# Softmax of head pairs 0 to 6 divided behind the mixing, and the first output weights split by ScalarE and VectorE

## The chip, the cores and the metric

One core of a Trainium2 chip runs the whole program. The metric is the device time of one execution in microseconds, the median over repeated runs. The core has five engines, each with an in-order queue of its own: TensorE (PE; its weight loads are listed as PEld), VectorE (DVE), ScalarE (ACT), GpSimd (POOL) and SyncE (SP), which issues most of the DMAs.

## What is computed

Two layers on x of 512 frames by 1024 channels, in fp32: a causal pooling mixer with a gated MLP, then chunked attention with a gated MLP. The change lies in the attention (16 heads of 64 channels; with 512 frames and chunks of 64 a frame sees its own chunk and all before it):

```python
def chunk_attention(h, w_qkv, q_norm, k_norm, rel_table, w_o):
    q, k, v = jnp.split(h @ w_qkv, 3, axis=-1)
    q = head_rmsnorm(q, q_norm)
    k = head_rmsnorm(k, k_norm)
    ...
    s = jnp.einsum('bqhd,bkhd->bhqk', qc, kb) * scale + bias
    s = jnp.where(valid, s, -1e30)
    p = jax.nn.softmax(s, axis=-1)
    o = jnp.einsum('bhqk,bkhd->bqhd', p, vb)
    ...
    return o @ w_o

x = x + chunk_attention(rmsnorm(x, g), ...)
```

Softmax divides each row of exp(s - max) by its sum. The division may stand ahead of the product with v, where it acts on 512 x 512 numbers of a head, or behind it, where it acts on 512 x 64.

## The kernel before

Nearly every fp32 operand of a matmul is split into a high and a low part (`split`, lines 96 to 103: the high part is a rounded copy, by default by ACT, line 102, the low part is the difference, by default by DVE, line 103). With `eng_hi` and `eng` another engine does them (line 100 for the high part). A product is then three matmuls (`mm3`, lines 123 to 125: high by high, high by low, low by high). `load_split` (lines 111 to 119) loads a 128 x 1024 block of weights by SP's queue (line 117) and splits it; raw blocks have three buffers, high and low parts two each.

The attention works on pairs of heads, `p` 0 to 7, since two heads of 64 channels fill 128 partitions. One loop of 68 steps runs over the 64 tiles (head, 128 queries): in step i come the scores of tile i (`scores`), the transposition of tile i - 2 (`turn`), and every fourth step the mixing of a whole head whose last tile is i - 4 (`mix`). Two steps in eight also turn q and k of the next pair (`channel_major`). Between them PE is given "fillers": the projection of the next q and k (up to step 35.5), and from there the first six pairs' part of the output product (`outputs`, 144 matmuls), spread evenly over the steps.

For one tile the chain is: PE's `sc` (lines 1394 and 1395); DVE adds the bias and takes the extreme into `mx` (line 1398); ACT makes Exp into `sb` and its row sum (line 1400); DVE makes 1/sum (line 1401); ACT multiplies `sb` by it (line 1402); PE turns `sb` with `ident` into `tp` (line 1410); ACT and DVE split `tp` into `pt0h`, `pt0l` (even heads) or `pt1h`, `pt1l` (odd heads; lines 102 and 103); PE mixes into `oo` (line 1422); ACT copies half of it as `ob` (line 1427) and DVE adds it into `O2[p]`, named `o` in the trace (line 1428). `O2[p]` is split into `XS[p]`, named `two` in the trace, and multiplies the output weights `wo_h`, `wo_l`.

The order of PE alone is written by hand in this loop. On the other engines, SP's queue too, a scheduler lays the instructions out from the same program. `sc`, `zt`, `tp`, `oo` take the four buffers of the S bank of PSUM in rotation. The output weights of the first six pairs come in six blocks of 128 x 1024; POOL makes their high and low parts (`load` in `output`).

Of the kernel before, what the change touches and what calls it, by code (L numbers as in the profile page):

```python
# [17 lines left out]
F32 = mybir.dt.float32  # L18
F32R = mybir.dt.float32r
AF = mybir.ActivationFunctionType  # L20
# [3 lines left out]
P = 128  # L24
S = 512
# [5 lines left out]
HD = 64  # L31
NPAIR = H // 2
TT = S // P
# [39 lines left out]
def trunk(ctx: ExitStack, tc: tile.TileContext, xt, xT, cols, band, edge, poolw, gv, wout, wqk, wv, wo, rel, out):  # L73
    nc = tc.nc
# [3 lines left out]
    tmp = ctx.enter_context(tc.tile_pool(name="tmp", bufs=1))  # L78
    dram = ctx.enter_context(tc.tile_pool(name="dram", bufs=1, space=bass.MemoryType.DRAM))
# [9 lines left out]
    def psum(tag, name, bufs=2):  # L89
        return ps.tile([P, S], F32, name=name, tag=tag, bufs=bufs)  # L90
# [30 lines left out]
    def mm3(o, sh, sl, mh, ml, first, last, **how):  # L121

        yield nc.tensor.matmul(o, sh, mh, start=first, stop=False, **how)  # L123
        yield nc.tensor.matmul(o, sh, ml, start=False, stop=False, **how)  # L124
        yield nc.tensor.matmul(o, sl, mh, start=False, stop=last, **how)  # L125
# [15 lines left out]
    def small(name, n, tag="nw"):  # L141
        return tmp.tile([P, n], F32, name=name, tag=f"{tag}{n}", bufs=4)
# [211 lines left out]
    ident = consts.tile([P, P], F32, name="ident")  # L354
    col = consts.tile([P, NCOL], F32, name="col")
    ones = consts.tile([P, 1], F32, name="ones")
    gq = consts.tile([P, 2], F32, name="gq")
    rdram = dram.tile([H, RLEN], F32, name="rdram")
    ET = mybir.EngineType
    with tc.tile_pool(name="start", bufs=1) as sp, tc.manual_schedule(engines={ET.PE, ET.DVE, ET.Activation, ET.Pool, ET.SP}):  # L360
        first, second, acc0 = mixer(sp)

    def ffn(l, first, pool, acc, summed=None, upool=None, hook=None):
# [56 lines left out]
        def early():  # L420
# [6 lines left out]
            for at, (f, k, i) in enumerate(units):  # L427
# [13 lines left out]
                if at == (19, 14)[l]:  # L441

                    order = tc.manual_schedule(engines={ET.DVE, ET.Activation}) if l == 0 else nullcontext()
                    order.__enter__()
# [388 lines left out]
        def tour():  # L833
# [8 lines left out]
            def place(f, k):  # L842

                for word in PLACES[k].split():
                    x, name = word.split(".")
                    step = steps_of(f + "qofn".index(x) - 2).get(name)
                    if step:
                        step()

            for f in range(KIND.index("s"), NF + 2):  # L850
# [10 lines left out]
                for k in range(7):  # L861
                    if (f, k) == (ORDERED, 0):
                        order.enter_context(tc.manual_schedule(engines={ET.DVE, ET.Activation, ET.SP}))
                    place(f, k)
# [50 lines left out]
    def attention(rest, hook, hidden_slots):  # L915
        XS = set2
        O2, V, Z, QK, SM = {}, {}, {}, {}, {}
# [407 lines left out]
        def output(ps_, after=None):  # L1325

            p0, p1 = ps_[0], ps_[-1] + 1
            n = (p1 - p0) * P
            nd = D // n
            w = {}  # L1330

            def load(d):
                eng = nc.gpsimd if p0 < 6 else None
                w[d] = load_split(wo[d:d + nd, :, p0 * P:p1 * P].rearrange("d p m -> p d m"), D, f"wo{d}_{p0}", eng=eng, eng_hi=eng)

            o, early = {}, 2 if p1 - p0 == 4 else 0
            order = [(d, p) for d in range(early) for p in ps_[:-1]] + [(d, p1 - 1) for d in range(early)]
            for d, p in order + [(d, p) for d in range(early, KD) for p in ps_]:
                if d - d % nd not in w:
                    load(d)  # L1340
                hi, lo = w[d - d % nd]
                if d not in o:
                    o[d] = psum("PQ"[d % 2], f"wo{d}_{p0}")
                s = slice(d % nd * n + (p - p0) * P, d % nd * n + (p - p0 + 1) * P)
                yield from mm3(o[d], hi[:, s], lo[:, s], XS[p], XS[KD + p], p == p0, p == p1 - 1)
                if p < p1 - 1:
                    continue
                nc.vector.tensor_add(X[d], o[d], X[d])
                if after:
                    after(d)  # L1350
                    if d == 1:
                        load(nd)
# [28 lines left out]
        def scores(h, t):  # L1381

            p, e = divmod(h, 2)
            q, k, kl = QK[p, 0][e], QK[p, 1][e], KL[p % 2][e]
            if t == 0:

                base = rdram[h, :]
                for r, n in ((0, S - HD), (HD, S)):
                    nc.sync.dma_start(BT[h % 2][r:r + HD, S - n:], bass.AP(tensor=base.tensor, offset=base.offset + HD, ap=[[1, HD], [1, n]]))
            n = (t + 1) * P  # L1390
            nw = max(n, 256)

            sc = psum("S", f"sc{h}_{t}", 4)
            nc.tensor.matmul(sc[:, :nw], q[:, t * P:n], k[:, :nw], start=True, stop=False)
            nc.tensor.matmul(sc[:, :nw], q[:, t * P:n], kl[:, :nw], start=False, stop=True)  # L1395
            SM[h, t] = s_ = heads.tile([P, n], F32, name=f"sb{h}_{t}", tag=f"sb{t}")
            mx = tmp.tile([P, 3], F32, name=f"mx{h}_{t}", tag="mx", bufs=4)
            nc.vector.tensor_tensor_reduce(out=s_[:, :n], in0=sc[:, :n], in1=BT[h % 2][:, :n][:, ::-1], scale=1.0,  # L1398
                                           scalar=3e38, op0=OP.add, op1=OP.min, accum_out=mx[:, 0:1])
            nc.scalar.activation(s_[:, :n], s_[:, :n], AF.Exp, scale=-1.0, bias=mx[:, 0:1], accum_out=mx[:, 1:2])  # L1400
            nc.vector.reciprocal(mx[:, 2:3], mx[:, 1:2])
            nc.scalar.activation(s_[:, :n], s_[:, :n], AF.Copy, scale=mx[:, 2:3])

        def turn(h, t):

# [7 lines left out]
        def mix(h):  # L1413

            p, e = divmod(h, 2)
            hs = slice(e * HD, (e + 1) * HD)
            oo = psum("S", f"oo{h}", 4)
            if p not in O2:
                O2[p] = heads.tile([P, S], F32, name=f"o2_{p}", tag="o2", bufs=4)
            for c in range(2):  # L1420
                for j in range(TT):
                    nc.tensor.matmul(oo[:, j * P:], V[j, h // 4][:, h % 4].rearrange("p a d -> p (a d)"),
                                     PT[e][c][:, 4 * j:3 * j + TT].rearrange("p t q -> p (t q)"),
                                     start=j == 0 and c == 0, stop=j == TT - 1 and c == 1)
            ob = g_tile(f"ob{h}")
            other = slice(HD - e * HD, 2 * HD - e * HD)
            nc.scalar.activation(ob[hs], oo[other], AF.Copy)
            nc.vector.tensor_add(O2[p][hs], oo[hs], ob[hs])

        r2, late = small("r2", TT), []  # L1430
        closing = ExitStack()
        with tc.tile_pool(name="pre", bufs=1, reuse_waits="tile") as pre:
            with tc.manual_schedule(engines={ET.PE, ET.DVE, ET.Activation, ET.SP}):
                rcol, second = opening(pre)
        heads = closing.enter_context(tc.tile_pool(name="bh", bufs=1, reuse_waits="tile"))
# [9 lines left out]
        with tc.manual_schedule(engines={mybir.EngineType.PE}):  # L1445
            cur, done, kept = 0, 0, 0

            def fill(upto):

                nonlocal cur, done  # L1450
                while cur < len(fillers):
                    g, n, a, b = fillers[cur]
                    due = n * (upto - a) / (b - a)
                    while done < min(due, n):
                        next(g)
                        done += 1
                    if upto < b:
                        return
                    run(g)
                    cur, done = cur + 1, 0  # L1460

            fill(0)
            for i in range(nb + LAG + LAGM):
                steps = []
                if i < nb:
                    steps.append(lambda: scores(*tiles_[i]))
                if i % 8 in CM and i // 8 + 1 < NPAIR:
                    steps.append(lambda: channel_major(i // 8 + 1, CM.index(i % 8)))
                j = i - LAG
                if 0 <= j < nb:  # L1470
                    steps.append(lambda: turn(*tiles_[j]))
                j2 = j - LAGM
                if 0 <= j2 < nb and j2 % TT == TT - 1:
                    steps.append(lambda: mix(tiles_[j2][0]))
                for x, step in enumerate(steps):
                    step()
                    if late and x < 2:
                        late.pop(0)()
                    fill(i + (x + 1) / len(steps))

                while 8 * kept + 7 <= j2 and (cur == 3 or cur == 2 and done >= 24 * (kept // 2 + 1)):
                    split(O2[kept], XS[kept], XS[KD + kept])
                    kept += 1
            fill(nb + FO)
# [97 lines left out]
```

## Time and profile before

| | |
|---|---|
| runs | 967.28 us (median of 3; 967.24 to 968.49) |
| profiled execution | 969.2 us, of which its span 967.4 |
| granted TensorE clock | 1.00 |
| attention loop, first scores to the last `sc` | 447.7 to 596.2 us |
| DMA | 103.87 MB, mean 107 GB/s |

The span is the time from the first to the last instruction; the rest of an execution lies around it. The rows on which the argument rests are quoted where they are used, in the prediction. A row of the timeline gives start, duration, engine, line, operation, out<-in, shape and count; behind it in brackets, the idle time of the engine just before it and what ended that. A row of a group gives count, busy time, mean ns of one, and idle time before.

### The profile page before, as it was taken

How to read it: one execution, taken by the hardware profiler on the slowest of the kernel's cores; microseconds unless marked ns; L12 is line 12 of the kernel's file. 1: busy time of each engine (PE TensorE's matmuls, PEld its weight loads, DVE VectorE, ACT ScalarE, POOL GpSimd, SP SyncE). 2: the span in 40 equal slices, each digit the busy share in tenths (PEclk: the TensorE clock that was granted, in tenths of full speed). 3: DMA queues.
4: the chain of work that ended last, by engine and by line, in shares of the span. 5: the costliest groups of instructions: out<-in, count | busy, mean ns of one | idle time of the engine just before them, and what ended most of it. 6: DMA issues, size and time to landing. Idle time of an engine off the chain costs nothing.

```text
span 967.4 us, 13737 instructions
## 1 busy us (share of the span) xinstructions
PE 956.3 (99%) x4958; PEld 810.0 (84%) x4958; DVE 849.5 (88%) x1522; ACT 594.0 (61%) x1023; POOL 91.2 (9%) x81
## 2 busy tenths in 40 slices
PE   8999999999999999999999999999999999999998
PEld 7788988888888888888888777888988888888886
DVE  8999999999899859895786887999999999989953
ACT  7665554655555457466898888656565565456531
POOL 2300000000000000043525441000000000000000
PEclk9999999999999999999999999999999999999999
DMA  9222332332323317024433341332333233332323
GB/s 343 73 97 71 115 108 81 120 120 80 114 79 120 102 48 292 21 66 133 132 113 97 88 117 55 100 109 80 94 115 108 84 120 111 102 104 79 114 79 111
DMA packets 38996, 103.87 MB, mean 107 GB/s; under 512 B 4464, under 2 KB 7936, under 8 KB 38928
## 3 DMA queue, kind: packets, MB, share of 16 engines
q1 hardware_dynamic: 38864, 102.95, 33.0%
q8 instruction: 39, 0.64, 0.3%
q14 instruction: 29, 0.24, 0.1%
q0 software_dynamic: 32, 0.04, 0.0%
q10 hardware_dynamic: 32, 0.00, 0.0%
HBM read 96.65 MB, written 2.14 MB: 102 GB/s over the span
## 4 chain that ended last, share of the span: by engine, by line
PE 87%; DVE 8%; ACT 2%; DMA 1%; issue 1%; SPq 0%; POOL 0%; DVEq 0%; ACTq 0%; POOLq 0%
PE st_m L593 10%; PE out L124 8%; PE out L125 8%; PE out L123 8%; PE st_m L595 5%; PE st_t L593 5%; PE gv L124 4%; PE gv L125 4%; PE gv L123 4%; PE qk L123 3%; PE qk L124 3%; PE qk L125 3%; PE st_t L595 3%; PE st_b L593 3%; PE tp L1410 1%; PE st_b L595 1%
## 5 line engine op out<-in xcount | busy, mean ns | idle before, releaser
L124 PE MATMUL out<-one,ow_h 128*128 128x512 f32 x224 | 88.1, 393 | 0.0
L123 PE MATMUL out<-one,ow_h 128*128 128x512 f32 x224 | 88.0, 393 | 0.0
L125 PE MATMUL out<-one,ow_l 128*128 128x512 f32 x224 | 87.9, 393 | 0.0
L829 DVE TENSOR_TENSOR X<-out,X 128x512 f32<-128x512 f32 (+1 forms) x65 | 44.3, 683 | 45.9 <-PE out L125 45.6
L593 PE MATMUL st_m<-two,g_h 128*128 128x512 f32 x240 | 75.1, 394 | 0.1
L593 PE MATMUL st_m<-h,g_h 128*128 128x512 f32 x240 | 74.1, 390 | 0.0
L392 ACT ACTIVATE ow_h<-wo_r 128x768 fp32r<-128x768 f32 (+1 forms) x56 | 44.4, 794 | 43.4 <-PE out L124 39.8
L407 DVE SCALAR_TENSOR_TENSOR c<-a,col,c 128x511 f32<-128x511 f32 (+1 forms) x76 | 56.8, 749 | 0.0
L593 PEld LDWEIGHTS st_m<-h,g_h 128*128 128x128 f32 x240 | 45.1, 188 | 10.3
L595 PEld LDWEIGHTS st_m<-two,g_l 128*128 128x128 f32 x240 | 45.0, 188 | 9.6
L593 PEld LDWEIGHTS st_m<-two,g_h 128*128 128x128 f32 x240 | 44.0, 188 | 10.4 <-ACT w L602 0.8
L393 DVE TENSOR_TENSOR ow_l<-wo_r,ow_h 128x768 fp32r<-128x768 f32 (+1 forms) x56 | 50.4, 899 | 2.3 <-ACT ow_h L392 2.3
L602 ACT ACTIVATE w<-st_m 128x512 f32<-128x512 f32 x30 | 18.0, 598 | 55.2 <-PE st_m L595 55.2
L595 PE MATMUL st_m<-h,g_l 128*128 128x256 f32 x240 | 48.3, 283 | 0.0
L595 PE MATMUL st_m<-two,g_l 128*128 128x256 f32 x240 | 47.6, 280 | 0.0
L124 PEld LDWEIGHTS out<-one,ow_h 128*128 128x128 f32 x224 | 42.4, 189 | 5.7 <-DVE one L418 0.3
L125 PEld LDWEIGHTS out<-one,ow_l 128*128 128x128 f32 x224 | 42.4, 189 | 5.5
L123 PEld LDWEIGHTS out<-one,ow_h 128*128 128x128 f32 x224 | 42.4, 189 | 5.4
L1398 DVE CUSTOM_DVE_ANT_0 sb<-sc,B 128x128 f32<-128x128 f32 (+1 forms) x64 | 31.1, 486 | 17.9 <-PE sc L1395 13.3
L404 ACT ACTIVATE c<-a,col 128x512 f32<-128x512 f32 x38 | 30.7, 813 | 23.8 <-DVE a L751 22.2
L392 ACT ACTIVATE g_h<-gv_r 128x1024 fp32r<-128x1024 f32 x32 | 33.7, 1055 | 13.5 <-DMA gv_r<-gv 12.9
L1400 ACT ACTIVATE sb<-sb,mx 128x128 f32<-128x128 f32 (+1 forms) x64 | 35.7, 558 | 9.8 <-DVE mx L1398 9.2
(459 smaller groups left out, 3035.7 us busy)
## 6 DMA issues: line engine op xcount, KB each, us to landing
gv_r<-gv SPq DMA_DIRECT2D x86, 512.0 KB, 3.9
wo_r<-wout SPq DMA_DIRECT2D x32, 384.0 KB, 3.1
wo_r<-wout SPq DMA_DIRECT2D x32, 320.0 KB, 2.9
wqk_r<-wqk SPq DMA_DIRECT2D x12, 512.0 KB, 3.5
b<-wv SPq DMA_DIRECT2D x8, 512.0 KB, 6.7
wo_r<-wo SPq DMA_DIRECT2D x8, 512.0 KB, 3.6
xt<-xt SPq DMA_DIRECT2D x4, 512.0 KB, 5.2
X<-xT SPq DMA_DIRECT2D x8, 256.0 KB, 7.5
```

The source lines that it names most:

```text
L123: yield nc.tensor.matmul(o, sh, mh, start=first, stop=False, **how)
L124: yield nc.tensor.matmul(o, sh, ml, start=False, stop=False, **how)
L125: yield nc.tensor.matmul(o, sl, mh, start=False, stop=last, **how)
L392: nc.scalar.activation(hi[:, :n], raw[:, :n], AF.Copy)
L393: return hi, lo, lambda: nc.vector.tensor_sub(lo[:, :n], raw[:, :n], hi[:, :n].bitcast(F32))
L404: nc.scalar.activation(c, a, AF.Identity, scale=cw[2], bias=cw[3])
L407: nc.vector.scalar_tensor_tensor(c[:, j:], a[:, :S - j], cw[2 - j], c[:, j:], op0=OP.mult, op1=OP.add)
L593: nc.tensor.matmul(o, hi[:, c], B[i, name], start=first and i == 0, stop=False, **how)
L595: nc.tensor.matmul(o[:, 0], lo[:, c], B[i, name][:, 0], start=False, stop=i == 3, **how)
L829: nc.vector.tensor_add(X[d][:, fs], o[:, fs], X[d][:, fs])
L1398: nc.vector.tensor_tensor_reduce(out=s_[:, :n], in0=sc[:, :n], in1=BT[h % 2][:, :n][:, ::-1], scale=1.0, scalar=3e38, op0=OP.add, op1=OP.m ...
L1400: nc.scalar.activation(s_[:, :n], s_[:, :n], AF.Exp, scale=-1.0, bias=mx[:, 0:1], accum_out=mx[:, 1:2])
```

## The change

For pairs 0 to 6 the multiplication by 1/sum on `sb` is left out. Exp writes its row sums into one tile of 128 x 8 for the pair (`sums`); after the eighth tile DVE inverts all eight columns at once. Two steps later (`sums_out`, step 8p + 9) PE turns this tile into 8 x 128 (`rt`, a fifth user of the S bank), ACT copies it (`rs`) and SP writes it to a DRAM tensor `rinv`. After two more steps (`sums_in`) SP reads it back, each head's 512 numbers broadcast over 64 partitions (`rb`), and after four more (`scale`) POOL multiplies `O2[p]` by it. `O2[p]` is split four steps later than before at the earliest and has three buffers in place of four. Pair 7 stays as it was. Besides, the six output weight blocks of the first pairs are split by ACT and DVE in place of POOL.

```diff
             def load(d):
-                eng = nc.gpsimd if p0 < 6 else None
+                eng = None
...
-            nc.scalar.activation(s_[:, :n], s_[:, :n], AF.Exp, scale=-1.0, bias=mx[:, 0:1], accum_out=mx[:, 1:2])
-            nc.vector.reciprocal(mx[:, 2:3], mx[:, 1:2])
-            nc.scalar.activation(s_[:, :n], s_[:, :n], AF.Copy, scale=mx[:, 2:3])
+            if p < NPAIR - 1:
+                if e == 0 and t == 0:
+                    sums[p] = tmp.tile([P, 2 * TT], F32, name=f"sums{p}", tag="sums", bufs=2)
+                c = e * TT + t
+                nc.scalar.activation(s_[:, :n], s_[:, :n], AF.Exp, scale=-1.0, bias=mx[:, 0:1], accum_out=sums[p][:, c:c + 1])
+                if c == 2 * TT - 1:
+                    nc.vector.reciprocal(sums[p], sums[p])
+            else:
+                nc.scalar.activation(s_[:, :n], s_[:, :n], AF.Exp, scale=-1.0, bias=mx[:, 0:1], accum_out=mx[:, 1:2])
+                nc.vector.reciprocal(mx[:, 2:3], mx[:, 1:2])
+                nc.scalar.activation(s_[:, :n], s_[:, :n], AF.Copy, scale=mx[:, 2:3])
+
+        def sums_out(p):
+
+            rt = psum("S", f"rt{p}", 4)
+            nc.tensor.transpose(rt[:2 * TT, :P], sums.pop(p), ident)
+            rs = heads.tile([2 * TT, P], F32, name=f"rs{p}", tag="rs")
+            nc.scalar.activation(rs, rt[:2 * TT, :P], AF.Copy)
+            nc.sync.dma_start(rinv[p], rs)
+
+        def sums_in(p):
+
+            RB[p] = heads.tile([P, S], F32, name=f"rb{p}", tag="rb")
+            for b in range(2):
+                nc.sync.dma_start(RB[p][b * HD:(b + 1) * HD], rinv[p, b * TT:(b + 1) * TT, :].rearrange("c q -> (c q)")[None].to_broadcast([HD, S]))
+
+        def scale(p):
+            nc.gpsimd.tensor_mul(O2[p], O2[p], RB.pop(p))
...
-                O2[p] = heads.tile([P, S], F32, name=f"o2_{p}", tag="o2", bufs=4)
+                O2[p] = heads.tile([P, S], F32, name=f"o2_{p}", tag="o2", bufs=3)
...
             for i in range(nb + LAG + LAGM):
                 steps = []
+                p = (i - 9) // 8
+                if 0 <= p < NPAIR - 1 and (i - 9) % 8 in (0, 2, 6):
+                    (sums_out, sums_in, scale)[(i - 9) % 8 // 2 - (i - 9) % 8 // 6](p)
...
-                while 8 * kept + 7 <= j2 and (cur == 3 or cur == 2 and done >= 24 * (kept // 2 + 1)):
+                while 8 * kept + (11 if kept < NPAIR - 1 else 7) <= j2 and (cur == 3 or cur == 2 and done >= 24 * (kept // 2 + 1)):
                     split(O2[kept], XS[kept], XS[KD + kept])
```

On PE the program before and after differ by the seven turns of sums alone. One of them, in step 57, before the change (`tp13_2` is head 13, tile 2; `wo6_0_h` the high part of the fourth block of output weights):

```order
L1410 MATMUL tp13_2_6069<-ident_106,sb13_2_6011 128x128 x3
L125 MATMUL wo6_0_6006<-two1_97,wo6_0_l_6002 128x512
L123 MATMUL wo7_0_6077<-two0_96,wo6_0_h_6001 128x512
L1394 MATMUL sc14_1_6079<-zh7_1_5930,zh7_0_5898 128x256
L1395 MATMUL sc14_1_6079<-kl10_3419,zh7_0_5898 128x256
L124 MATMUL wo7_0_6077<-two4_100,wo6_0_h_6001 128x512
```

and after it:

```order
L1436 MATMUL tp13_2_6026<-ident_106,sb13_2_5968 128x128 x3
L125 MATMUL wo6_0_5963<-two1_97,wo6_0_l_5959 128x512
L123 MATMUL wo7_0_6034<-two0_96,wo6_0_h_5958 128x512
L1416 MATMUL rt6_6036<-ident_106,sums6_5812 8x128
L1395 MATMUL sc14_1_6041<-zh7_1_5893,zh7_0_5860 128x256
L1396 MATMUL sc14_1_6041<-kl10_3420,zh7_0_5860 128x256
L124 MATMUL wo7_0_6034<-two4_100,wo6_0_h_5958 128x512
```

The turn of the sums of pair 6 stands just ahead of the scores of head 14, tile 1, and takes a buffer of the S bank from the rotation.

On ACT, in pair 4 (head 9), before the change (line 1400 is Exp, line 1402 the scaling, `two1_97` the high part of pair 3's result):

```order
L102 ACTIVATE two1_97<-o2_3_5352 128x512
L102 ACTIVATE pt0h_4302<-tp8_3_5560 128x4x128
L1400 ACTIVATE sb9_1_5552,mx9_1_5553<-sb9_1_5552,mx9_1_5553 128x256
L1402 ACTIVATE sb9_0_5518<-sb9_0_5518,mx9_0_5519 128x128
L102 ACTIVATE pt1h_4304<-tp9_0_5581 128x128
L135 ACTIVATE qk3_t_4989<-qk3_a_4987 128x32
L136 ACTIVATE qk3_y_4988<-qk3_t_4989 128x32
L1400 ACTIVATE sb9_2_5573,mx9_2_5574<-sb9_2_5573,mx9_2_5574 128x384
L1402 ACTIVATE sb9_1_5552<-sb9_1_5552,mx9_1_5553 128x256
L1400 ACTIVATE sb9_3_5590,mx9_3_5591<-sb9_3_5590,mx9_3_5591 128x512
L1402 ACTIVATE sb9_2_5573<-sb9_2_5573,mx9_2_5574 128x384
```

and after it (line 1405 is Exp):

```order
L102 ACTIVATE pt0h_4303<-tp8_3_5527 128x4x128
L1405 ACTIVATE sb9_1_5521,sums4_5346<-sb9_1_5521,mx9_1_5522 128x256
L102 ACTIVATE two1_97<-o2_3_5322 128x512
L102 ACTIVATE pt1h_4305<-tp9_0_5546 128x128
L1405 ACTIVATE sb9_2_5540,sums4_5346<-sb9_2_5540,mx9_2_5541 128x384
L135 ACTIVATE qk3_t_4972<-qk3_a_4970 128x32
L102 ACTIVATE pt1h_4305<-tp9_1_5563 128x2x128
L136 ACTIVATE qk3_y_4971<-qk3_t_4972 128x32
L1405 ACTIVATE sb9_3_5556,sums4_5346<-sb9_3_5556,mx9_3_5557 128x512
```

The three scalings of head 9 are gone from between the Exps, and the high part of pair 3's result has moved behind the Exp of head 9, tile 1.

On POOL, at the end of the loop, before the change (`wo6_0`, `wo0_4` and `wo4_4` are the last three blocks of output weights, the casts turn a half of the keys or queries of pairs 6 and 7):

```order
L1375 CAST z26_1_5714<-zh6_1_5713 64x512
L100 CAST wo6_0_h_6001<-wo6_0_r_6000 128x1024
L103 TENSOR_TENSOR wo6_0_l_6002<-wo6_0_r_6000,wo6_0_h_6001 128x1024
L1375 CAST z27_0_5899<-zh7_0_5898 64x512
L1375 CAST z27_1_5931<-zh7_1_5930 64x512
L100 CAST wo0_4_h_6147<-wo0_4_r_6146 128x1024
L103 TENSOR_TENSOR wo0_4_l_6148<-wo0_4_r_6146,wo0_4_h_6147 128x1024
L100 CAST wo4_4_h_6273<-wo4_4_r_6272 128x1024
L103 TENSOR_TENSOR wo4_4_l_6274<-wo4_4_r_6272,wo4_4_h_6273 128x1024
```

and after it:

```order
L1376 CAST z26_1_5682<-zh6_1_5681 64x512
L1428 TENSOR_TENSOR o2_4_5570<-o2_4_5570,rb4_5665 128x512
L1376 CAST z27_0_5861<-zh7_0_5860 64x512
L1376 CAST z27_1_5894<-zh7_1_5893 64x512
L1428 TENSOR_TENSOR o2_5_5780<-o2_5_5780,rb5_5877 128x512
L1428 TENSOR_TENSOR o2_6_5998<-o2_6_5998,rb6_6078 128x512
```

The casts and subtractions of output weights have left POOL's queue; the multiplications of the results of pairs 4, 5 and 6 stand there now.

More of the change, by code (lines that the diff above doesn't have):

```diff
@@ L358, in trunk @@
     rdram = dram.tile([H, RLEN], F32, name="rdram")
+    rinv = dram.tile([NPAIR, 2 * TT, P], F32, name="rinv")
     ET = mybir.EngineType
@@ L1428, in mix @@
             nc.vector.tensor_add(O2[p][hs], oo[hs], ob[hs])
-        r2, late = small("r2", TT), []
+        r2, late, sums, RB = small("r2", TT), [], {}, {}
         closing = ExitStack()
```

## Prediction

> **What bounds the kernel now.** The first view is the profile's page: how much of the span TensorE (PE) works.
>
> ```profile
> span 967.4 us, 13737 instructions
> PE 956.3 (99%) x4958; PEld 810.0 (84%) x4958; DVE 849.5 (88%) x1522; ACT 594.0 (61%) x1023; POOL 91.2 (9%) x81
> ```
>
> PE is busy for 99% of the span, so whatever the change takes from ScalarE (ACT) or VectorE (DVE) is worth only what PE waits for them. The change lives in the attention loop, 440 to 604 us. The second view is the busy time of each engine in three stretches of it (columns: PE, weight loads, DVE, ACT, POOL, each with its count; clock; DMA share; GB/s).
>
> ```profile
> 440.00:540.00 100.00, 100.00 (x541) 84.28 (x540) 69.01 (x211) 84.78 (x205) 43.23 (x33) 1.00 0.37 112
> 540.00:570.00 30.00, 28.52 (x165) 23.41 (x164) 25.08 (x82) 26.56 (x70) 14.45 (x11) 1.00 0.39 111
> 570.00:604.00 34.00, 31.31 (x172) 25.14 (x171) 28.78 (x75) 26.90 (x68) 8.08 (x6) 1.00 0.22 62
> ```
>
> PE never stands still up to 540 us (pairs 0 to 3), although ACT is busy for 85 of those 100 us; behind 540 it stands still for 1.48 + 2.69 = 4.2 us. The change can win only there. The third view is whom PE waited for in the loop (total, times, longest), the fourth the PE timeline at those places, each hold with the row ahead of it.
>
> ```profile
> PE tp L1410 <- ACT sb L1402: 3.2, 5, 1.7
> PE oo L1422 <- DVE pt1l L103: 0.5, 1, 0.5
> PE sc L1394 <- DMA zh<-zh: 0.3, 1, 0.3
> ```
>
> ```profile
> 540.33 0.40 PE L123 MATMUL wo<-two,wo_h 128*128 128x512 f32 x1
> 540.85 0.52 PE L1410 MATMUL tp<-ident,sb 128*128 128x128 f32 x3
> ...
> 543.62 0.39 PE L124 MATMUL wo<-two,wo_h 128*128 128x512 f32 x1
> 543.85 0.40 PE L125 MATMUL wo<-two,wo_l 128*128 128x512 f32 x1
> 544.50 0.33 PE L1410 MATMUL tp<-ident,sb 128*128 128x128 f32 x1 [0.25 <-ACT sb L1402]
> ...
> 545.84 0.40 PE L123 MATMUL wo<-two,wo_h 128*128 128x512 f32 x1
> 547.05 0.44 PE L1410 MATMUL tp<-ident,sb 128*128 128x128 f32 x2 [0.82 <-ACT sb L1402]
> ...
> 564.48 0.40 PE L124 MATMUL wo<-two,wo_h 128*128 128x512 f32 x1
> 565.17 0.35 PE L1394 MATMUL sc<-zh,zh 128*128 128x256 f32 x1 [0.30 <-DMA zh<-zh]
> ...
> 578.84 0.40 PE L123 MATMUL wo<-two,wo_h 128*128 128x512 f32 x1
> 580.89 0.43 PE L1410 MATMUL tp<-ident,sb 128*128 128x128 f32 x2 [1.65 <-ACT sb L1402]
> ...
> 586.77 0.40 PE L123 MATMUL wo<-two,wo_h 128*128 128x512 f32 x1
> 587.33 0.33 PE L1410 MATMUL tp<-ident,sb 128*128 128x128 f32 x1 [0.17 <-ACT sb L1402]
> ```
>
> Matmuls overlap, so I price a hold by starts: 543.62 to 543.85 shows that the next start follows a 512-column matmul after 0.23 us. Beyond that the holds cost 0.52 - 0.23 = 0.3 (540.85), 0.65 - 0.23 = 0.4 (544.50), 1.21 - 0.23 = 1.0 (547.05), 0.69 - 0.23 = 0.5 (565.17), 2.05 - 0.23 = 1.8 (580.89) and 0.56 - 0.23 = 0.3 (587.33): **4.3 us**. The first five lie in pairs 4 to 6 (heads 8 to 13), where the change acts. 587.33 is head 14, whose scaling stays, but ACT's new order puts that scaling ahead of the next tile's Exp. The wait of the last mixing for `pt1l` stays.
>
> **What goes.** ACT's scaling of the probabilities (line 1402) is left out for 56 of 64 tiles, and `tp` then waits for Exp alone, two instructions earlier in the chain (no 1/sum, no scaling). That takes the holds at 540.85, 544.50 and 547.05. The big one has a cause of its own:
>
> ```profile
> 577.29 2.92 DVE L103 TENSOR_TENSOR two<-o,two 128x512 fp32r<-128x512 f32 x1
> 577.28 2.38 POOL L103 TENSOR_TENSOR wo_l<-wo_r,wo_h 128x1024 fp32r<-128x1024 f32 x1
> 580.32 0.51 ACT L1402 ACTIVATE sb<-sb,mx 128x256 f32<-128x256 f32 x1 [2.15 <-DVE mx L1401]
> 594.23 0.68 DVE L103 TENSOR_TENSOR two<-o,two 128x512 fp32r<-128x512 f32 x1
> ```
>
> The subtraction `two<-o,two` takes 2.92 us where the same one takes 0.68 at 594.23; POOL's `wo_l` had begun 0.01 us before it and ran 2.38. Behind it stood 1/sum, then ACT's scaling, then PE. The change removes POOL's `wo_l`, and head 13's 1/sum and scaling too, so this hold goes twice over. The Trainium skill ("SBUF — State Buffer", Who interferes with whom) says that a DVE instruction with two SBUF inputs and a GpSimd instruction that reads SBUF exclude each other for the whole instruction, the first to start winning. The two rows agree (2.38 + 0.68 = 3.06, measured 2.92). That rule also speaks against the change: six more two-input subtractions now run on DVE, and POOL gets seven multiplications that read SBUF; by it a bad meeting costs a hold again, which is the third rival below. The hold at 565.17 waits for a DMA of pair 6 that was issued behind a `wo_r` load; that load now goes ahead of pair 6's four moves and POOL's cast no longer queues behind `wo_l`, so I count it as gone. In all **-4.3 us**.
>
> **What comes.** Seven transposes of the sums on PE. The nearest row is the single transpose `tp` with its neighbours:
>
> ```profile
> 569.28 0.48 PE L125 MATMUL wo<-two,wo_l 128*128 128x512 f32 x1
> 569.59 0.27 PE L1410 MATMUL tp<-ident,sb 128*128 128x128 f32 x1
> 569.62 0.47 PE L123 MATMUL wo<-two,wo_h 128*128 128x512 f32 x1
> 569.93 0.39 PE L124 MATMUL wo<-two,wo_h 128*128 128x512 f32 x1
> ```
>
> From 569.28 to 569.93 there are two 512-column starts and one transpose: 0.65 - 2 x 0.23 = 0.19 us. 7 x 0.19 = **+1.3 us**, of which four fall before 540 us where nothing can pay for them. The bounds are 0 (hidden in a hold) and 7 x 0.27, the transpose's own duration, = 1.9.
>
> The transpose takes one of the four rotating S banks, and that moves the score matmul right behind it onto the bank of `oo` of the step before, so it waits for the addition of `oo` on DVE:
>
> ```profile
> 549.75 0.68 DVE L1428 TENSOR_TENSOR o<-oo,ob 64x512 f32<-64x512 f32 x1
> 550.57 0.28 PE L1394 MATMUL sc<-zh,zh 128*128 128x256 f32 x1
> ```
>
> Here the addition ends 0.14 us before that matmul starts (550.43 against 550.57): just in time. Over seven pairs I put 0 to 0.3 us each and take 0.4 together.
>
> Six splits of output weights move from POOL to ACT and DVE. The group of ACT's scalings (count, busy time, mean, idle before), the same splits where ACT and DVE do them already, and POOL's multiplication:
>
> ```profile
> L1402 ACT ACTIVATE sb<-sb,mx 128x128 f32<-128x128 f32 (+1 forms) x64 | 35.5, 556 | 3.8 <-DVE mx L1401 3.0
> ```
>
> ```profile
> 601.34 1.06 ACT L102 ACTIVATE wo_h<-wo_r 128x1024 fp32r<-128x1024 f32 x1
> 602.73 1.22 DVE L103 TENSOR_TENSOR wo_l<-wo_r,wo_h 128x1024 fp32r<-128x1024 f32 x1
> 547.54 4.05 POOL L1321 TENSOR_TENSOR z<-z,qk_y 128x512 f32<-128x512 f32 x4 [5.17 <-DVE qk_y L1319]
> ```
>
> ACT gets 6 x 1.06 = 6.4 us and loses 56 scalings of 0.556 = 31; DVE gets 6 x 1.22 = 7.3 and loses 56 small 1/sums, so DVE does not get lighter where they stand, and each `wo_l` stands ahead of score work in its queue. Two steps of the loop lie between a tile's scores and its transposition, which covers 1.2 us nearly everywhere. The exception is pair 7: its scaling stays, and ACT's last `wo_h` stands ahead of an Exp of head 14 and waits for PE to free its buffer. That chain would be up to 0.8 us late over a few tiles; bounds 0 and 6 x 1.22 = 7.3 (every split shows in full). I take 0.5, near the lower end, because each split has steps of cover.
>
> The division itself (PE, ACT copy, DMA out, two DMAs in, POOL multiplication) I cost at nothing. The nearest DMAs are a write to and a read from DRAM:
>
> ```profile
> rdram<-rs POOLq DMA_DIRECT2D x1, 39.9 KB, 2.4
> B<-rdram SPq DMA_DIRECT2D x16, 128.0 KB, 3.1
> ```
>
> About 1.5 us to the issue, 2.4 out, 0.5 for the second issue, 3.1 in and 4.05/4 = 1.0 to 2.38/2 = 1.2 on POOL: some 8.5 us. The loop takes 164 / 68 = 2.4 us a step. Pair 3, whose result PE asks for soonest, has seven steps, 17 us, from its transposition to that. Pair 6 has the least:
>
> ```profile
> 584.56 0.28 PE L1394 MATMUL sc<-zh,zh 128*128 128x256 f32 x1
> 594.26 0.58 ACT L102 ACTIVATE pt0h<-tp 128x512 fp32r<-128x512 f32 x1
> ```
>
> Its transposition comes just ahead of the score matmul at 584.56, so its chain ends near 593.1, and ACT's split of its result comes behind the `pt0h` that ends at 594.84. On SP's queue the two reads wait for the write and hold up what follows, `wo_r` loads and the moves of the next pair, by up to 3 us; those moves have 4 us or more until their scores, so nothing is added.
>
> **Sum:** -4.3 + 1.3 + 0.4 + 0.5 = -2.1 us. The profiled execution took 969.2 us with a span of 967.4; the median of the runs is 967.28, 1.9 below that execution. On the median: 967.28 - 2.1 = **965.2 us**.
>
> **Rivals.**
> - *More*: the new waits do not appear, transposes cost half: -4.3 + 0.7 = -3.6, 963.7 us. For it: ACT is freed of 31 - 6 = 25 us. Against: DVE is not.
> - *The holds come back elsewhere*: DVE with its six `wo_l` becomes the late engine in pairs 4 to 7 and PE waits for it about 3 us in all: -4.3 + 1.3 + 3.0 = 0, 967.3 us. For it: DVE is busy 85% behind 570 us (28.78 of 34) and has no gap of 1.22 us in most steps. Against: two steps of cover.
> - *DVE and POOL meet again*: one of POOL's multiplications runs under a DVE subtraction at a place without slack and costs up to the 1.8 us of 580.89: -2.1 + 1.8, 967.0 us. For it: the rows at 577. Against: POOL loses six subtractions of 2.38 us (14 us, and six casts) and gets 7 x 1.2 = 8, so meetings are rarer.
> - *Slower*: the division of pair 6 comes late. ACT's split of its result stands ahead of two scalings of head 15 that PE waits for. It has 594.8 - 593.1 = 1.7 us to spare; each further microsecond goes to the end of the loop one for one. The whole is slower than before from 1.7 + 2.1 = 3.8 us late, by over 0.2% from 5.7 us late; at 6.5 us it gives 965.2 + 4.8 = 970.0 us. For it: six steps on five engines in a row. A landing of 6.3 us, as one DMA had here, would do half of it.
>
> ```profile
> DMA to landing us min/median/max: 2.2/2.6/6.3
> ```
>
> That row is the landing times of the score operands' moves (14 `zh` DMAs). Against: the median of 2.6.
> - That the change does not do what it says: the holds were set by PE's order or by Exp, and `tp` waits the same without the scaling. The row at 580.32 shows ACT idle for 2.15 us on 1/sum, which speaks against it; it would give 967.28 + 1.3 = 968.6.
>
> **How the numbers follow.** About 0.2% (1.9 us) is what a measurement of this kernel can tell from no change, so the line for faster is 965.35. Forecast (964.5 to 966.2) 0.42; more 0.16; holds elsewhere 0.18; meeting again 0.08; slower 0.10; no effect 0.06. Faster takes the 0.16 and some 0.34 of the forecast, whose centre is just over the line: 0.50. Slower than 969.2: 0.10. The rest: 0.40. The range 963.4 to 968.0 leaves out the upper cases and little below.
>
> **What would show it.** Right: PE's wait list without `sb`, or with pair 7's alone; no DVE subtraction of 2.9 us near 577; PE idle of some 2 us in 540 to 604 us instead of 4.2; seven `rt` rows of about 0.2 us. Wrong: PE waiting for `o` or `oo` ahead of the `rt` or the score matmul behind it; PE waiting for DVE behind a `wo_l`; ACT waiting for POOL at `two<-o`; idle time before 540 us.

## The result and the profile after

| | median, us | runs | against before |
|---|---|---|---|
| before | 967.28 | 5 (966.46 to 968.49) | |
| after | 972.19 | 5 (971.88 to 973.68) | 1.0051, 95% interval [1.0036, 1.0066] |

The change makes the kernel **4.9 us slower**. The prediction was 965.2 us, with a range that ended at 968.0. The profiled execution of after took 972.28 us; this is the head of its page:

```profile
span 970.5 us, 13715 instructions
PE 960.2 (99%) x4965; PEld 809.0 (83%) x4965; DVE 849.1 (87%) x1479; ACT 575.0 (59%) x980; POOL 80.5 (8%) x76
```

ACT has 19 us less to do and POOL 11 us less, as the change says. PE's busy time has risen by 3.9 us for 7 more matmuls. The three stretches of the attention loop, in the columns of the table shown for before:

```profile
440.00:540.00 100.00, 100.00 (x540) 83.94 (x540) 66.58 (x182) 71.52 (x177) 41.84 (x31) 1.00 0.40 122
540.00:570.00 30.00, 28.11 (x163) 22.86 (x162) 27.84 (x71) 22.52 (x59) 9.45 (x9) 1.00 0.43 130
570.00:604.00 34.00, 32.50 (x186) 26.88 (x185) 28.70 (x76) 27.07 (x67) 3.81 (x4) 1.00 0.27 83
```

PE now stands still for 1.89 us between 540 and 570 (1.48 before) and for 1.50 behind 570 (2.69 before): 0.8 us less than in the execution that was predicted from, where 2 were forecast. In another execution of before (run 5 below) PE stands still for 2.2 us in these stretches, and against that one the change loses 1.2. The holds on PE's timeline in those stretches, the idle time before each in brackets with what ended it:

```profile
555.72 0.33 PE L1365 MATMUL zt<-ident,z 128*128 128x128 f32 x1 [1.65 <-POOL z L1322]
...
588.95 0.44 PE L1436 MATMUL tp<-ident,sb 128*128 128x128 f32 x2 [0.26 <-ACT sb L1411]
599.21 0.55 PE L1436 MATMUL tp<-ident,sb 128*128 128x128 f32 x3 [0.69 <-ACT sb L1411]
603.21 0.85 PE L1448 MATMUL oo<-pt1l,one 128*128 128x512 f32 x4 [0.55 <-DVE pt1l L103]
```

The listed `sb` holds in pairs 4 to 6 are gone. The first row is new: PE waits for `z`, q and k of the next pair, normed by POOL. And behind the last row stands something that no wait explains. The same row on before's timeline:

```profile
602.87 0.84 PE L1422 MATMUL oo<-pt1l,one 128*128 128x512 f32 x4 [0.55 <-DVE pt1l L103]
```

From that start to the end of the span before has 967.4 - 602.87 = 364.5 us and after 970.5 - 603.21 = 367.3, for the same instructions at a granted clock of 1.00 in both. PE hardly stands still there; its matmuls start further apart. Ahead of the loop it is the same, in the stretch from 40 to 240 us, first of before, then of after:

```profile
40.00:240.00 200.00, 200.00 (x1074) 172.24 (x1074) 193.74 (x310) 116.82 (x171) 0.00 (x0) 1.00 0.30 99
```

```profile
40.00:240.00 200.00, 200.00 (x1069) 171.11 (x1068) 193.32 (x310) 116.67 (x171) 0.00 (x0) 1.00 0.30 99
```

PE is busy for all of it in both, with 1074 matmuls and with 1069.

### The profile page after: what moved, and what is told of

It reads as the page before. It is cut to its first block, busy times and chain, and to the rows that moved or that the text cites. A ratio compares the mean times of both kernels' runs of the same rounds, so it can differ in the third digit from the quotient of the medians.

```text
span 970.5 us, 13715 instructions
## 1 busy us (share of the span) xinstructions
PE 960.2 (99%) x4965; PEld 809.0 (83%) x4965; DVE 849.1 (87%) x1479; ACT 575.0 (59%) x980; POOL 80.5 (8%) x76
## 5 line engine op out<-in xcount | busy, mean ns | idle before, releaser
L1405 ACT ACTIVATE sb<-sb,mx 128x128 f32<-128x128 f32 (+3 forms) x56 | 31.3, 559 | 17.8 <-DVE mx L1399 16.8
```

## The experiments

Three theories stood at the start. **A**: the two new `sums` tiles (2 x 32 bytes of every partition, in the pool `tmp`) move what is laid out behind them by 64 bytes, and PE's matmuls take longer there. **B**: the order in the loop, with the late `z`. **C**: the trip of 1/sum through DRAM. From the built programs' layout:

```
            before    after
sums0            -   141824
xt0, h0     141824   141888
xt1, h1     145920   145984
```

### 1. The kernel before with 64 bytes more

```diff
     tmp.tile([P, 32], F32, name="fill1")
+    tmp.tile([P, 16], F32, name="fill2")
```

> The kernel before with one more tile of 64 bytes a partition that nobody reads or writes; every tile laid out behind it starts 64 bytes further on, and no instruction differs. Theory A (the loss is the place of the tiles: the change's two sums tiles move what lies behind them by 64 bytes, and TensorE's matmuls outside the attention loop then start some 1 ns further apart): 3 to 5 us slower than before, 970.5 to 972.5, with the mean step of a matmul outside the loop about 1 ns longer. Theory B (the loss is in the attention loop's order: the late z and its 1.65 us hold): no difference, 967.3 within 0.5. Theory C (the trip of the inverse sums through DRAM or their place in DRAM): no difference either.

Measured: 970.95 us, 1.0036 [1.0024, 1.0049], so +3.5 us by the ratio, from a tile that no instruction touches. Its last mixing and its span:

```profile
span 968.9 us, 13737 instructions
...
601.95 0.85 PE L1423 MATMUL oo<-pt1l,one 128*128 128x512 f32 x4 [0.55 <-DVE pt1l L104]
```

968.9 - 601.95 = 367.0 us for the stretch that takes 364.5 in before. Theory A holds as a cause; whether it is all of the loss, the next three say.

### 2 to 4. The change with its tiles in their old places, and each half of it alone

Run 2 is the whole change with one word altered, run 4 the same with POOL's weights kept (its expectation counts the pairs 0 to 6 from 1), run 3 only the weights:

```diff
-  sums[p] = tmp.tile([P, 2 * TT], F32, name=f"sums{p}", tag="sums", bufs=2)
+  sums[p] = heads.tile([P, 2 * TT], F32, name=f"sums{p}", tag="sums", bufs=2)
```

> The whole change with the sums tiles laid out in the pool of the heads, so that the tiles that lay behind them in the other pool stand where they stood before. Theory A (place of the tiles): 3 to 5 us faster than the changed kernel, 967 to 969. Theory B (order in the loop): as the changed kernel, 972.2 within 0.7. Theory C (the trip through DRAM): as the changed kernel, 972.2 within 0.7.

> The kernel before with only the second part of the change: hi and lo of the first output weights by ScalarE and VectorE. No sums tile, no trip through DRAM. Theory A (place of the tiles): 966 to 968, the four POOL split holds go (about -3) and the 1.65 us hold of TensorE on z comes with the weights' lo on VectorE. Theory B (order in the loop): if the late z is what costs, 970 to 972. Theory C: as before or faster, 965 to 967.5.

> The kernel before with only the first part of the change (pairs 1 to 7 divided behind the mixing), the sums tiles in the pool of the heads, and the first output weights' hi and lo left to POOL. Theory A (place of the tiles): 967 to 969, as before but for 7 transposes of 0.09 us and the holds that POOL's weights make. Theory B (the late z comes from the weights on VectorE): 967 to 969 as well. Theory C (the trip through DRAM slows what runs beside it): 970 to 972.

Measured: run 2 969.46 us (1.0023 [1.0015, 1.0032]), run 3 969.68 (1.0026 [1.0016, 1.0035]), run 4 969.71 (1.0023 [1.0014, 1.0032]), beside a median of 967.24 for before. So by the medians the place of the tiles is 2.7 us of the loss, and 2.2 us remain to the loop. Runs 3 and 4 lie in none of the ranges that were expected of them. Run 2's profile has the span back behind the loop, and the hold on `z` is where it was in after:

```profile
span 966.5 us, 13715 instructions
...
554.36 0.33 PE L1365 MATMUL zt<-ident,z 128*128 128x128 f32 x1 [1.65 <-POOL z L1322]
...
601.90 0.85 PE L1448 MATMUL oo<-pt1l,one 128*128 128x512 f32 x4 [0.52 <-DVE pt1l L103]
```

966.5 - 601.90 = 364.6, as before. The halves don't add up: each alone costs as much as both. The weights alone do not make the hold on `z`, against what was expected of run 3; they bring holds on `sb` instead. POOL starts on `z` as late in run 3 as in run 2 (549.11 and 549.27), but takes 4.05 us there and not 5.03. The division alone has two of its own, in pairs 4 to 6, on ACT's `pt1h` and on a score bank that DVE frees:

```profile
547.80 0.41 PE L1436 MATMUL tp<-ident,sb 128*128 128x128 f32 x2 [1.11 <-ACT pt1h L102]
568.54 0.39 PE L1395 MATMUL sc<-zh,zh 128*128 128x256 f32 x1 [0.59 <-DVE mx L1399]
```

For theory C there is no sign: run 2 has the trip through DRAM and run 3 hasn't, and they take the same; and after's list of waits has none of PE, ACT or DVE for the divided result.

### 5. The kernel before, profiled once more

Nothing is changed here. In run 1, which has before's instructions to the letter, the hold at 580.89 us was missing.

> The kernel before, nothing changed, for a second profiled execution. Theory D (the profiled execution of before, 969.2 us where the median is 967.2, had a hold of its own: TensorE's 1.7 us for ScalarE's sb at 580.89, which the typical execution hasn't, so that the prediction took off time that isn't there): a profile of 966.5 to 967.8 us without a hold over 1 us between 540 and 604. Rival (the hold is in every execution and the 1.9 us lie elsewhere): the hold of about 1.7 us at 580 to 582 again.

Measured: 967.13 us (1.0003 [0.9993, 1.0013]); the profiled execution took 966.59, with this timeline of PE's holds behind 540 us, and this meeting of DVE and POOL:

```profile
span 964.8 us, 13737 instructions
```

```profile
544.42 0.33 PE L1410 MATMUL tp<-ident,sb 128*128 128x128 f32 x1 [0.23 <-ACT sb L1402]
546.97 0.44 PE L1410 MATMUL tp<-ident,sb 128*128 128x128 f32 x2 [0.83 <-ACT sb L1402]
584.74 0.33 PE L1410 MATMUL tp<-ident,sb 128*128 128x128 f32 x1 [0.19 <-ACT sb L1402]
596.28 0.55 PE L1410 MATMUL tp<-ident,sb 128*128 128x128 f32 x3 [0.28 <-ACT sb L1402]
600.26 0.84 PE L1422 MATMUL oo<-pt1l,one 128*128 128x512 f32 x4 [0.54 <-DVE pt1l L103]
```

```profile
576.67 0.68 DVE L103 TENSOR_TENSOR two<-o,two 128x512 fp32r<-128x512 f32 x1
576.69 2.92 POOL L103 TENSOR_TENSOR wo_l<-wo_r,wo_h 128x1024 fp32r<-128x1024 f32 x1
```

This is the row of 2.92 us on which the prediction's largest term stood, the other way round. In the execution that was predicted from, POOL started at 577.28 and DVE at 577.29: DVE took 2.92 us, POOL 2.38, and PE waited 1.65. Here DVE started 0.02 us ahead: DVE takes 0.68, POOL takes the 2.92, and PE doesn't wait, since nothing hurries for `wo_l`. The six profiled executions of before's instructions (before, 1, 5, 6, 7 and 9) all have the two starts within 0.02 us; POOL was first in two of them (before and 6), and these two have the hold (1.65 and 1.66 us). That the first to start holds off the other for its whole length is what the Trainium skill says ("SBUF — State Buffer", Who interferes with whom), and all six agree. The hold at 565.17 on a DMA isn't in run 5 either. What stays in it are the holds of 0.23, 0.83, 0.19 and 0.28 us and the last mixing's wait.

### 6 and 7. How far the tiles must be moved

As run 1 with 128 and with 256 bytes (`[P, 32]` and `[P, 64]`).

> As the padded kernel of 64 bytes, with 128 bytes. Theory A in the form that a matmul's operands must begin at a multiple of 128 bytes: no loss, 967.3 within 0.6, steps of 227 ns. In the form that it is a multiple of 512 (in before the few operands at 384 above a multiple of 512 already take steps of 231 to 235 ns): 3 to 5 us slower, steps of 231 to 233 ns. Rival (a displacement of any size costs, by the tiles' place against each other): slower too.

> As the padded kernel of 64 bytes, with 256 bytes. Multiple of 128 or of 256 is enough: no loss, 967.3 within 0.6. Multiple of 512: 3 to 5 us slower, steps of 231 to 233 ns. Rival (a displacement of any size costs): slower too; if 128 bytes cost nothing and 256 cost as much as 64, neither form holds.

Measured: with 128 bytes 970.30 us, 1.0037 [1.0023, 1.0050]; with 256 bytes 966.55 us, 0.9997 [0.9988, 1.0006]. The tiles moved in all three cases against those ahead of the filler, so it isn't the move; it is the place. Neither of the two forms of theory A came out: 128 bytes cost time, so a multiple of 128 isn't enough, and 256 cost none, so it needn't be one of 512. Counted from the addresses in the programs, these matmuls have an operand that doesn't begin at a multiple of 256 bytes:

| kernel | such matmuls (the profile of before has 4958 in all) | last mixing to the end, us | median against before |
|---|---|---|---|
| before | 544 | 364.5 | |
| 64 bytes (run 1) | 3356 | 367.0 | 1.0036 |
| 128 bytes (run 6) | 3220 | 366.5 | 1.0037 |
| 256 bytes (run 7) | 544 | 364.6 | 0.9997 |
| after | 3359 | 367.3 | 1.0051 |
| change, sums in `heads` (run 2) | 691 | 364.6 | 1.0023 |

In run 1 that makes 3.5 us / (3356 - 544) = 1.2 ns for each. Behind the loop it falls on the 512-column matmuls. Their steps from one start to the next, worked out from the traces' start times over 605 to 960 us (steps of 150 to 300 ns; "on": this moving operand and the next weights both begin at a multiple of 256):

```
                    on: count  mean ns  median    off: count  mean ns  median
before                  1155    229.1     227            77    232.6     232
run 1,  64 bytes         305    229.9     230           917    232.3     233
run 6, 128 bytes         347    229.9     229           878    231.8     232
run 7, 256 bytes        1155    229.1     227            77    232.8     232
```

The steps that count as "on" are longer in runs 1 and 6 too, 230 ns in the median against 227. The two operands that were classed here don't explain that, and it stays open.

### 8. The late z

On the way to the hold at 555.72 us in after stand these rows, of DVE and POOL:

```profile
542.40 1.22 DVE L103 TENSOR_TENSOR wo_l<-wo_r,wo_h 128x1024 fp32r<-128x1024 f32 x1
546.25 0.18 DVE L1317 TENSOR_TENSOR qk_a<-qk_s,r 128x32 f32<-128x32 f32 x1
550.37 0.19 DVE L1320 TENSOR_TENSOR qk_y<-qk_y,n_y 128x32 f32<-128x32 f32 x1
553.08 1.68 DVE L103 TENSOR_TENSOR wo_l<-wo_r,wo_h 128x1024 fp32r<-128x1024 f32 x1
```

```profile
550.63 5.03 POOL L1322 TENSOR_TENSOR z<-z,qk_y 128x512 f32<-128x512 f32 x4 [4.53 <-DVE qk_y L1320]
```

DVE's new `wo_l` of 1.22 us stands ahead of the chain `qk_a` to `qk_y`; POOL's four multiplications of `z` start at 550.63 (547.54 in before; half of the difference is the 1.5 us by which after is late already at 530) and take 5.03 us, not 4.05: the last of the four, beside the next `wo_l`, takes 2.02 us in place of 1.04, and that `wo_l` 1.68 in place of 1.22. Run 8 is run 2 with that one load given back to POOL:

```diff
-                eng = None
+                eng = nc.gpsimd if d == 2 and p0 == 0 else None
```

> The change with the sums tiles in the pool of the heads, and one of the six loads of the first output weights (the second, whose lo on VectorE stood at 541 us between the squares' sums and the norm of z) given back to POOL for hi and lo. Theory (the rest of the loss is the hold on z at 555 us, 2.1 us later than in the padded kernel, made by that lo): 967.0 to 968.0, the hold on z gone, about 2 us faster than with the sums tiles alone moved. Rival (the hold on z is covered by another wait that comes next, or the remaining 2.2 us are the 7 transposes and what waits behind them): 969 to 970.

Measured: 968.23 us, 1.0015 [1.0005, 1.0024], 1.2 us faster than run 2, where 2 were expected. The hold on `z` is gone. Two others have come in its place, and a meeting of DVE and POOL made by the cure:

```profile
543.84 2.26 DVE L1317 TENSOR_TENSOR qk_a<-qk_s,r 128x32 f32<-128x32 f32 x1
```

```profile
543.65 2.41 POOL L103 TENSOR_TENSOR wo_l<-wo_r,wo_h 128x1024 fp32r<-128x1024 f32 x1
```

```profile
547.06 0.41 PE L1436 MATMUL tp<-ident,sb 128*128 128x128 f32 x2 [1.12 <-ACT pt1h L102]
554.90 0.50 PE L1395 MATMUL sc<-zh,zh 128*128 128x512 f32 x1 [0.42 <-DVE mx L1399]
```

A DVE instruction of 0.18 us takes 2.26, until POOL's `wo_l` ends at 546.06. In before that `wo_l` ran at 539.97; here POOL's new multiplication of `o` stands ahead of it. The profiled executions of the two runs don't differ so: their spans are 966.5 us (run 2) and 966.8 (run 8). Where the 1.2 us of the medians come from is taken up with run 13.

### 9 to 11, and 13. Aligned tiles, before and after

Three fillers (128 bytes at the front of the pool `tmp`, 128 by a wider `mx`, 224 ahead of the pool on the right side) bring the matmuls off a multiple of 256 to 88 in before and 95 with the change. Run 13 is the change with these fillers, run 10 also has run 8's load on POOL, run 11 the last load of the output weights too:

```diff
     tmp.tile([P, 32], F32, name="fill1")
+    tmp.tile([P, 32], F32, name="fill2")
...
-            mx = tmp.tile([P, 3], F32, name=f"mx{h}_{t}", tag="mx", bufs=4)
+            mx = tmp.tile([P, 16], F32, name=f"mx{h}_{t}", tag="mx", bufs=4)
...
+    hidden_slots.enter_context(tc.tile_pool(name="bf", bufs=1, side="right")).tile([P, 56], F32, name="fill3")
```

(That is run 9; with the change, `sums` is made `[P, 16]` wide in place of `mx`.) In run 11 `eng = nc.gpsimd if (p0, d) in ((0, 2), (4, 4)) else None`.

> The kernel before with three fillers, so that the matmuls with an operand that doesn't begin at a multiple of 256 bytes fall from 544 to 88 (they are 3356 with 64 bytes of filler, 3220 with 128, 544 with 256). Theory A (each such matmul costs about 3.6 us / 2815 = 1.3 ns): 456 x 1.3 ns = 0.6 us faster, 966.2 to 967.0. Rival (the loss belongs to the tiles that moved, not to the multiple of 256): no difference, 967.1 within 0.3.

> The change with the second load of the output weights given back to POOL and the same three fillers (95 matmuls off a multiple of 256 instead of 691). Theory A: 0.6 to 0.8 us faster than the unaligned one of 968.2, so 967.4 to 967.7. Rival: 968.2 within 0.4.

> As the one before, and the last load of the output weights given back to POOL too (the hold of TensorE on pair 7's scaling at 597.65, 0.68 us, stands behind that load's hi on ScalarE; with the weights on POOL it is not there). Theory: 0.4 to 0.7 us faster than the one before, about 967.0, level with before; faster than before only if the last 0.7 us of PE waits at 547 us go as well. Rival (POOL's lo meets VectorE's subtraction there and gives it back): no gain or up to 2 us slower.

> The change as it is, with the three fillers and nothing else (95 matmuls off a multiple of 256 instead of 3359). Theory A: 0.5 to 1.3 us faster than the change with the sums tiles in the pool of the heads (969.5, 691 such matmuls), so 968.2 to 969.0; beside the aligned kernel before (965.6) the change alone is then worth +2.6 to +3.4, by the late z (1.2) and by the transposes and the waits at 546, 553 and 597 us. Rival (no more than the place of the tiles): 965.6 within 0.7.

| run | median, us | against before |
|---|---|---|
| 9, before aligned | 965.57 | 0.9985 [0.9976, 0.9994] |
| 13, change aligned | 968.90 | 1.0015 [1.0006, 1.0024] |
| 10, and the second load on POOL | 967.29 | 1.0005 [0.9996, 1.0014] |
| 11, and the last load on POOL | 966.44 | 0.9994 [0.9985, 1.0003] |

Run 9 is faster than both kernels. It gained 1.3 us where 0.6 was expected: paired by start times, its trace gains 0.75 between 300 and 420 us, in the output product of the first MLP, where 192 matmuls of 512 columns with the moving operand at 224 above a multiple of 256 were put right, 3.9 ns each. The price of 1.2 ns was a mean over all shapes, and those were of the dear one. By the medians, the change as it is costs 968.90 - 965.57 = 3.3 us on aligned tiles; the second load gives back 1.6, the last one 0.85, and 0.9 is left.

The 1.6 and the 3.3 are not PE's waits alone. Six of run 13's eleven executions had a granted clock of 0.998 and took 968.9 to 969.7 us; the five at 1.00 took 967.2 to 968.2. In run 2 it is five at 0.998 (970.1 to 971.0) and six at 1.00 (968.4 to 969.5); in runs 8, 10 and 11 together it is one of 33. Among the executions at 0.999 or more, the change as it is costs 1.8 us on aligned tiles, and the second load gives back 0.15 (13 against 10) or 0.7 (2 against 8). No trace of an execution at 0.998 was kept, so what lowers its clock isn't shown; run 12 shows one way.

In run 10 PE still waits for pair 7's scaling, behind the last load's high part on ACT:

```profile
596.40 0.55 PE L1437 MATMUL tp<-ident,sb 128*128 128x128 f32 x3 [0.70 <-ACT sb L1412]
```

In run 11 there is no such row. The profiles of runs 8, 10 and 11 have a hold that no other has, far behind the loop: PE waits 0.30, 0.42 and 0.56 us for ACT's `v` at 900 us, in the second MLP. Why is open.

### 12. Without the seven transposes

```diff
-            rt = psum("S", f"rt{p}", 4)
-            nc.tensor.transpose(rt[:2 * TT, :P], sums.pop(p), ident)
-            rs = heads.tile([2 * TT, P], F32, name=f"rs{p}", tag="rs")
-            nc.scalar.activation(rs, rt[:2 * TT, :P], AF.Copy)
-            nc.sync.dma_start(rinv[p], rs)
+            nc.sync.dma_start(rinv[p].rearrange("c q -> q c"), sums.pop(p))
```

> As e11_aligned_d2_last, but the inverse sums go to DRAM by one DMA of 128x8 single numbers and are not turned by TensorE nor copied by ScalarE. Theory (TensorE pays about 0.1 us for each of the 7 transposes, with no wait on the S banks beside it): 0.6 to 0.8 us faster than that kernel's 966.4, so about 965.7, level with the aligned kernel before. Rival (the transposes lie beside other work and the remaining 0.9 us are the holds at 546 and 553): 966.4 within 0.3. Rival (the DMA of 1024 single numbers is late or in the way of the other transfers): slower than 967.

Measured: 976.48 us, 1.0097 [1.0083, 1.0111], 10 us slower than run 11. The issue's group (KB each, median us to landing), ACT's split of a pair's result, and PE:

```profile
rinv<-sums SPq DMA_DIRECT2D x7, 4.0 KB, 8.8
```

```profile
566.26 0.63 ACT L103 ACTIVATE two<-o 128x512 fp32r<-128x512 f32 x1 [4.99 <-POOL o L1425]
```

```profile
567.43 0.69 PE L1433 MATMUL tp<-ident,sb 128*128 128x128 f32 x2 [4.24 <-ACT sb L1406]
```

The write of 1024 single numbers lands after 8.8 us, and SP issues the first read of it 8.0 to 11.6 us behind the write; in after, whose profile has no landing for the write of eight rows, it does so 1.2 to 3.5 us behind. The division is late, ACT and DVE stand behind it in their queues, and PE waits 4.24 us: the mechanism of the prediction's slower rival, which in after itself has no wait. A second hold follows, and behind both the granted clock falls (two stretches, in the columns of the tables above; the clock is the third number from the end):

```profile
589.53 0.35 PE L1396 MATMUL sc<-zh,zh 128*128 128x256 f32 x1 [1.70 <-DVE pt1l L104]
```

```profile
567.00:573.00 6.00, 5.57 (x19) 4.79 (x20) 4.52 (x11) 3.65 (x10) 0.00 (x0) 0.52 0.60 138
590.00:594.00 4.00, 4.00 (x17) 3.26 (x16) 2.54 (x8) 1.62 (x5) 0.00 (x0) 0.59 0.55 111
```

By these rows some 6.0 x 0.48 + 4.0 x 0.41 = 4.5 of the 10 us are the clock and not the waits themselves (an estimate). The hold of 1.65 us on `z` in the profiles of after, 2 and 13 has no such fall behind it.

The run still prices the transposes. Ahead of any such wait, from 440 to 520 us, PE loses nothing against the aligned kernel before, where run 11 loses 0.12 us a pair. Behind the waits it says nothing of them.

## Why the prediction was wrong

Start times of the same PE instruction in two traces, less those of run 5 (in us, at five places of run 5's time; each column is the median over the 10 us that begin there):

| | 440 | 530 | 560 | 600 | 960 |
|---|---|---|---|---|---|
| before, the profile predicted from | 0.06 | 0.08 | 0.61 | 2.63 | 2.60 |
| 64 bytes (run 1) | 1.80 | 1.69 | 1.70 | 1.68 | 4.06 |
| after | 1.31 | 1.60 | 2.76 | 2.95 | 5.59 |
| change, sums in `heads` (run 2) | -0.18 | 0.22 | 1.44 | 1.65 | 1.65 |
| before aligned (run 9) | -1.34 | -1.32 | -1.33 | -1.32 | -1.42 |
| best with the change (run 11) | -0.42 | 0.01 | 0.84 | 0.43 | 1.16 |

Point by point:

- *"-4.3", what goes.* This is the step that failed first. The row `before` above steps up by 0.5 at 565 us and by 2.0 at 580 against the other execution: of the 4.3 us the holds at 565.17 and 580.89 (0.5 + 1.8 in the sum) belonged to the one execution, and some 4.3 - 2.5 = 1.8 us could be had. The holds from 540 to 547 did go, as forecast: run 2 stands at 0.22 at 530 and at -0.75 over 545 to 555. The hold on `z`, which the sum has no term for, then takes it to 1.44 at 560.
- *"On the median: 967.28 - 2.1".* The execution stood 1.9 us above the median, the prediction said so, and yet took its holds off the median. The excess was made of these holds: run 5's profiled execution lacks both and took 966.59 us where that one took 969.2. By its own terms with the real holds, -1.8 + 1.3 + 0.4 + 0.5, the sum would have been +0.4.
- *No term for the layout.* The prediction priced instructions, waits and queues, and took 64 bytes for nothing. They are 2.7 us of the 4.9 by the medians (after against run 2; 3.3 among executions at a clock of 0.999 or more, 3.9 between the two profiles at 960 in the table), and 3.5 in before (run 1). This is the largest part of the loss.
- *The `wo_l` on DVE, "0.5 ... pair 7".* The place was right: the last load costs 0.85 (run 11 against 10). But the sum took the cover as two steps of scores for all six and forgot what else is in DVE's queue: the second load stood ahead of the norm of `z`. By the medians that load is worth 1.2 us (run 8 against 2) to 1.6 (run 10 against 13), at an equal clock 0.7 and 0.15: in runs 8 and 10 the holds of 1.12 and 0.42 us stand where the 1.65 on `z` was.
- *"+1.3" and "+0.4", transposes and the bank behind them.* Too high: 0.12 us a pair for both where it can be read, which makes 0.8 for seven (an estimate). The group in after:

```profile
L1416 PE MATMUL rt<-ident,sums 128*8 128x128 f32 x7 | 1.9, 271 | 0.0
```

- *The division at nothing.* Right: no wait of PE, ACT or DVE for it in after; run 12 shows what it costs when late.
- *DVE and POOL meet again*, the rival at 967.0: the mechanism was right, twice (`wo_l` of 1.68 us beside POOL's 5.03 in after, `qk_a` of 2.26 us in run 8); the place wasn't, and in after it was POOL's late `z` and not a late DVE that PE waited for.

Of 4.9 us, then, 2.7 are the tiles' place by the medians, 1.2 the second load on DVE, and 1.0 what is left. Only the first is shown by itself, and at an equal clock it is more. How the other 2.2 us divide among the late `z`, the clock of 0.998, the last load's high part on ACT, the seven transposes and the `sb` holds that did go is argued and not settled. Why before's `sb` hold at 547 comes back as a hold on `pt1h` (1.12 us) as soon as `z` is early was seen as the meeting at 543.84, and not tried by itself. Neither is it settled why the weights alone cost 2.4 us; their profile shows holds on `sb` of 0.85, 0.27, 0.94, 0.23 and 0.49 us and two on DVE of 0.42 and 0.47, and how many of these every execution has is open.

## What to carry to other kernels

Profile the kernel before more than once, or at least ask which hold makes up the distance between the profiled execution and the median, before a change is credited with removing it: which of two instructions comes first, when they start within 0.02 us of each other, can differ from one execution to the next. Look at the granted clock of every execution before two medians are subtracted. A new small tile is a change to every tile behind it: give it a filler so that what PE streams keeps its multiple of 256 bytes. And when work is moved to a busy engine in program order, look for the short instructions behind it that another engine waits for, not for the engine's share of busy time.

## What the runs showed of the hardware

- Matmuls with an operand at 64, 128 or 224 bytes above a multiple of 256 take longer steps: 231.8 to 232.8 ns against 229.1 to 229.9 at 512 columns; 64 bytes cost 3.5 us in 967, 256 bytes nothing.
- DVE and POOL: an overlap decided by 0.01 to 0.02 us decides which of the two waits (0.68 us on DVE and 2.92 on POOL against 2.92 and 2.38), and with it 2.0 of the 2.6 us between the spans of two executions of the same kernel, 964.8 and 967.4 us.
- A DMA of 128 x 8 single numbers to DRAM landed after 8.8 us (median of run 12), and the read that waited for it was issued 8.0 to 11.6 us behind it; with the same 4 KB as 8 rows (after) the read was issued 1.2 to 3.5 us behind.
- In run 12 TensorE's granted clock was 0.52 over 567 to 573 us, behind a hold of 4.24 us, and 0.59 over 590 to 594, behind one of 1.70. Behind holds of 1.65 us (after, runs 2 and 13) it stayed at 1.00.
